# One core, a decoder layer in split fp32: the order of the first transfers, more work on two chunks behind the norms, and a second SwiGLU whose combinations read x from DRAM

## The chip, the cores and the metric

The kernel runs on one core of a Trainium2 chip. The time is device microseconds of one execution; below it is the median of three runs. The core has a matrix engine (PE, with its weight loads shown as PEld), a vector engine (DVE), a scalar engine (ACT), a third general engine (POOL), and an engine that mostly issues DMAs (SP). ACT and POOL issue DMAs too. Each engine takes its own instructions strictly in order and waits for the others by semaphores.

## The reference, cut to what matters

One step of a one-layer hybrid decoder for a prompt of 1024 tokens and 8 single-token samples that share the weights:

```python
def swiglu(x, w1, w3, w2):
    return (jax.nn.silu(x @ w1) * (x @ w3)) @ w2

def decoder_layer(x, ...):
    x = layer_norm(ALPHA * x + 0.5 * swiglu(x, ffn1_w1, ffn1_w3, ffn1_w2), ln1_g, ln1_b)
    m, st = hybrid_mixer(x, ...)      # x @ w_in -> RG-LRU and gated DeltaNet -> @ w_o
    x = layer_norm(ALPHA * x + m, ln2_g, ln2_b)
    x = layer_norm(ALPHA * x + 0.5 * swiglu(x, ffn2_w1, ffn2_w3, ffn2_w2), ln3_g, ln3_b)
    return x, st
```

x is 1032 x 1024, the hidden width of a SwiGLU is 2816, all in float32. The mixer's projection w_in gives, among others, K, Q and V of eight heads of 128, each followed by a causal convolution over time and a SiLU, and two gates per head.

## The kernel before, in words

**Number format and tiles.** Features lie on the 128 partitions, tokens along the free axis. The 1032 tokens are three chunks of 344 (`NT`, `TC`); the 1024 features are eight k-tiles (`KD`). A float32 operand is split into a rounded half and the rest (`split`: ACT writes the first, DVE or POOL subtracts): x into `XH`, `XL`, weights into `wh`, `wl`. Each product takes three matmuls per k-tile (`mm3`), so one output tile of 128 x 344 is a group of 24 matmuls.

**A SwiGLU** (`ffn`, run with n = 1 and n = 2) has 22 f-tiles of 128 hidden features. The first two (`FIRST`) are *plain*: w1 and w3, three chunks, 6 groups, 144 matmuls. Tiles 2 to 20 use *Strassen*: 7 products instead of 8 on blocks of 128 x 258, 168 matmuls. These need four linear combinations of quarters of x, split again into `CH` and `CL` (`combos`, four rounds k = 0 to 3). A round makes four tiles of x (`G`, or `u` and `si`) as XH + XL, one addition of 128 x 516 each on POOL, combines them on DVE, and splits the results (ACT, then DVE). `CL` lies in the memory of `ACC`. The tiles of a f-tile's result go to DRAM (`gs`, from POOL's queue) and are read back for w2. Tile 21 is plain, in the second half.

**The start.** `x_load(t)` loads the eight k-tiles of one chunk of x into `ACC` and splits them; chunk 0 from ACT's queue, chunks 1 and 2 from SP's, where the weights are loaded as well (`wload`, raw tiles of 128 x 512, three buffers).

**A norm** (class `LN`) runs per chunk in three steps: sums by matmuls with ones (`ps_sq`) give the mean and then the variance, and the last step scales and shifts and writes XH and XL. Four of the eight k-tiles (`ON_POOL`) are subtracted on POOL. The last chunk of a norm meets the stage that follows: `fin` is stepped from inside the mixer's first projections (`kqv_first`) and from the first plain tile of the second SwiGLU.

**The mixer** begins with K and Q of head 0 on chunks 0 and 1, then the gates' projections (`ab`), then chunk 2; then `gates()`, and V's three chunks behind it. Then come eight heads (`gdn`), with the projections of the next head as filler between them (`stream`). In head 0 the part that inverts a triangular matrix (line 848) is the next place with long dependencies. The order on each engine comes from the order in which the code is written, with a scheduler that moves instructions of one engine past one another unless they are pinned (`keep_in_program_order`).

**Beside the second SwiGLU** run sixteen jobs on the samples' states (`states`): two loads from POOL's queue each, four scalings on ACT and four on DVE.

## Time and profile before

| what | value |
|---|---|
| median of 3 runs | 2636.21 us (2635.96 to 2637.09) |
| the profiled execution | 2637.03 us, span of its instructions 2635.1 us |
| PE busy | 2535.4 us, 96% of the span |
| DVE, ACT, POOL busy | 1784.2, 1133.9, 493.8 us |
| chain that ended last | PE 80%, DVE 9%, ACT 7% of the span |
| granted TensorE clock, mean | 0.984 |

The span is the time from the first to the last instruction; the profiled execution's own time is 1.9 us longer. "Busy" of PE says that matmuls were in flight, also when the granted clock was low, so it is an upper bound of useful work. The page's forty slices are 65.9 us each.

### The profile page before, as it was taken

How to read it: one execution, taken by the hardware profiler on the slowest of the kernel's cores; microseconds unless marked ns; L12 is line 12 of the kernel's file. 1: busy time of each engine (PE TensorE's matmuls, PEld its weight loads, DVE VectorE, ACT ScalarE, POOL GpSimd, SP SyncE). 2: the span in 40 equal slices, each digit the busy share in tenths (PEclk: the TensorE clock that was granted, in tenths of full speed). 3: DMA queues.
4: the chain of work that ended last, by engine and by line, in shares of the span. 5: the costliest groups of instructions: out<-in, count | busy, mean ns of one | idle time of the engine just before them, and what ended most of it. 6: DMA issues, size and time to landing. Idle time of an engine off the chain costs nothing.

```text
span 2635.1 us, 47251 instructions
## 1 busy us (share of the span) xinstructions
PE 2535.4 (96%) x18398; PEld 2486.9 (94%) x18398; DVE 1784.2 (68%) x3657; ACT 1133.9 (43%) x2419; POOL 493.8 (19%) x612
## 2 busy tenths in 40 slices
PE   7999999999989999999999999999699999999996
PEld 7999999999979999999999999989699999999996
DVE  7766665645589676777767686767786666666446
ACT  4433333312363737465564637634533333332125
POOL 5000000300332021111112021144521111021013
PEclk8999999999989999999999999999899999999998
DMA  4222222423101121111211121123314444333221
GB/s 140 78 77 82 80 76 70 125 79 113 41 26 51 34 56 43 39 48 34 57 37 53 34 56 36 52 87 117 83 66 112 118 123 119 93 112 110 81 69 65
DMA packets 146816, 195.98 MB, mean 74 GB/s; under 512 B 34720, under 2 KB 75680, under 8 KB 146592
## 3 DMA queue, kind: packets, MB, share of 16 engines
q1 hardware_dynamic: 125024, 154.13, 19.3%
q0 software_dynamic: 10160, 32.06, 4.7%
q10 hardware_dynamic: 11408, 6.77, 0.9%
q8 instruction: 145, 2.38, 0.4%
q14 instruction: 79, 0.65, 0.1%
HBM read 156.15 MB, written 36.76 MB: 73 GB/s over the span
## 4 chain that ended last, share of the span: by engine, by line
PE 80%; DVE 9%; ACT 7%; issue 2%; POOL 1%; DMA 1%; ACTq 0%; SPq 0%; POOLq 0%; DVEq 0%
PE ps_mm L130 32%; PE ps_g L130 11%; PE ps_g L287 10%; PE ps_mm L287 10%; PE ps_sq L287 8%; ACT L88 2%; DVE ACC L94 2%; PE ps_g L848 2%; PE ps_sq L734 2%; DVE ACC L91 1%; ACT lnq L88 1%; DVE wl L91 1%; PE ps_g L734 1%; PE ps_g L740 1%; DMA ACC<-x 1%
## 5 line engine op out<-in xcount | busy, mean ns | idle before, releaser
L130 PE MATMUL ps_mm<-XH,wh 128*128 128x344 f32 x1680 | 568.9, 339 | 11.0 <-ACT XH L88 7.0
L130 PE MATMUL ps_mm<-XL,wh 128*128 128x344 f32 x1680 | 542.2, 323 | 6.2 <-POOL XL L91 6.1
L130 PE MATMUL ps_mm<-XH,wl 128*128 128x344 f32 x1680 | 542.7, 323 | 4.6 <-DVE wl L91 4.6
L88 ACT ACTIVATE wh<-wraw 128x512 fp32r<-128x512 f32 (+2 forms) x366 | 217.8, 599 | 423.2 <-PE ps_mm L130 155.4
L130 PEld LDWEIGHTS ps_mm<-XH,wh 128*128 128x128 f32 x1680 | 320.6, 191 | 15.3 <-ACT XH L88 7.6
L130 PEld LDWEIGHTS ps_mm<-XL,wh 128*128 128x128 f32 x1680 | 320.7, 191 | 8.9 <-POOL XL L91 6.9
L130 PEld LDWEIGHTS ps_mm<-XH,wl 128*128 128x128 f32 x1680 | 320.0, 190 | 5.7 <-DVE wl L91 5.6
L91 DVE TENSOR_TENSOR wl<-wraw,wh 128x512 fp32r<-128x512 f32 (+3 forms) x345 | 246.4, 718 | 52.5 <-ACT wh L88 47.4
L287 PE MATMUL ps_g<-CH,wh 128*128 128x258 f32 x760 | 214.7, 283 | 0.0
L287 PE MATMUL ps_g<-CH,wl 128*128 128x258 f32 x760 | 214.6, 282 | 0.0
L287 PE MATMUL ps_g<-CL,wh 128*128 128x258 f32 x760 | 214.3, 282 | 0.0
L88 ACT ACTIVATE wh<-S 128x512 fp32r<-128x512 f32 x152 | 95.8, 631 | 201.0 <-PE ps_sq L287 129.3
L287 PE MATMUL ps_mm<-XH,wl 128*128 128x258 f32 x608 | 171.5, 282 | 0.7 <-DVE wl L91 0.7
L287 PE MATMUL ps_mm<-XH,wh 128*128 128x258 f32 x608 | 171.8, 282 | 0.5 <-ACT wh L88 0.5
L287 PE MATMUL ps_mm<-XL,wh 128*128 128x258 f32 x608 | 171.3, 282 | 0.0
L342 POOL DMA_DIRECT2D gs<-G x76 | 41.5, 546 | 666.1 <-DVE G L91 618.9
L91 DVE TENSOR_TENSOR wl<-S,wh 128x512 fp32r<-128x512 f32 x152 | 105.0, 691 | 69.4 <-ACT wh L88 69.0
L287 PEld LDWEIGHTS ps_g<-CL,wh 128*128 128x128 f32 x760 | 143.5, 189 | 0.0
L287 PEld LDWEIGHTS ps_g<-CH,wh 128*128 128x128 f32 x760 | 143.2, 188 | 0.0
L287 PEld LDWEIGHTS ps_g<-CH,wl 128*128 128x128 f32 x760 | 143.1, 188 | 0.0
L88 ACT ACT_TABLE_LOAD x109 | 139.8, 1283 | 6.1 <-issue 3.3
L130 PE MATMUL ps_g<-gl,wh 128*128 128x344 f32 x444 | 142.1, 320 | 0.0
(503 smaller groups left out, 6872.5 us busy)
## 6 DMA issues: line engine op xcount, KB each, us to landing
wraw<-w SPq DMA_DIRECT2D x164, 256.0 KB, 2.8
wraw<-w_in SPq DMA_DIRECT2D x128, 256.0 KB, 2.6
gr<-gs SPq DMA_DIRECT2D x84, 258.0 KB, 2.8
gs<-G POOLq DMA_DIRECT2D x76, 258.0 KB, 2.6
wr<-w SPq DMA_DIRECT2D x76, 256.0 KB, 2.6
wraw<-w_o SPq DMA_DIRECT2D x40, 256.0 KB, 2.7
y<-ACC SPq DMA_DIRECT2D x32, 129.0 KB, 1.9
d<-lt SPq DMA_DIRECT2D x8, 512.0 KB, 3.3
```

The costliest lines, as they stand in the source:

```text
L88: return S.activation(out, in_, f, **kw)
L91: return (eng or V).tensor_tensor(out, a, b, op=op)
L94: return V.scalar_tensor_tensor(out, a, s, b, op0=op0, op1=op1)
L130: PE.matmul(p, a, b, start=(n == 0), stop=(n == 3 * nk - 1))
L287: PE.matmul(ps_[c], a[:, k, :], b, start=(start and n == 0), stop=(n == 11), skip_group_check=not start)
L342: G.dma_start(gs[f][:, s], x)
L734: x = PE.matmul(ck(p, i), a, b, start=True, stop=True)
L740: x = PE.transpose(ck(p, i), a, IDT)
L848: pin(PE.matmul(o[r, c, :], a(c), b(c), start=True, stop=True))
```

## The change

Three places are edited.

*Start of the first SwiGLU.* Chunk 0 of x is issued alternately from ACT's and POOL's queue; w1 and w3 of tile 0 are issued on SP ahead of chunks 1 and 2, pinned; w3's raw tiles come from the buffers `wr`, which the Strassen tiles use later; the splits of x are separated from its loads. The rounds of `combos` no longer add XH and XL: they load x from DRAM, rounds 0 and 1 from SP, rounds 2 and 3 from POOL's queue.

*Start of the mixer.* V of head 0 joins K and Q: its weights wait in the tiles `hM`, `hP`, `hLT`, `hP2`, and its convolution's input lies in the tile `lt`.

*Second norm and second SwiGLU.* The last step of the second norm writes y = the full x on ACT for all eight k-tiles, splits it, and stores it to DRAM (`X2`) from POOL's queue. `FIRST` becomes 3 for n = 2, so tile 2 is plain. Tiles 0 and 1 run on chunks 0 and 1 first, then both on chunk 2; tile 1's weights wait in the tiles of `S`, `wr`, `s0` and `rb`. The rounds of `combos` load x from `X2` on POOL's queue. What is left of the samples' jobs after the last Strassen tile is run there.

```diff
--- before.py
+++ after.py
@@ -25,7 +25,7 @@
 LN_EPS = 1e-5
 RMS_EPS = 1e-6
 NF = 22
-FIRST, LASTF = 2, 21
+FIRST, LASTF = {1: 2, 2: 3}, 21
 GROUPS = [[21, 0, 1], [2, 3, 4], [5, 6, 7, 8], [9, 10, 11, 12], [13, 14, 15, 16], [17, 18, 19, 20]]
 TH_ = T // 2
 TQ = T // 4
@@ -105,18 +105,20 @@
 
     LNB = {"s1": 3, "mu": 1, "s2": 2, "lnq": 3}
 
-    def wload(src, nk, m=128, eng=None, hold=None):
+    def wload(src, nk, m=128, eng=None, hold=None, raws=None, pin=False):
         hl = []
         for k0 in range(0, nk, 4):
             n = min(4, nk - k0)
             pad = [128, 512 // m, m]
-            raw = wp.tile([128, n, m], F32, name="wraw", tag="wraw", bufs=3, padded_shape=pad)
+            raw = raws() if raws else wp.tile([128, n, m], F32, name="wraw", tag="wraw", bufs=3, padded_shape=pad)
             if hold:
                 h, l = hold(n)
             else:
                 h = wp.tile([128, n, m], F32R, name="wh", tag="wh", bufs=4, padded_shape=pad)
                 l = wp.tile([128, n, m], F32R, name="wl", tag="wl", bufs=4, padded_shape=pad)
-            nc.sync.dma_start(raw, src[:, k0:k0 + n])
+            x = nc.sync.dma_start(raw, src[:, k0:k0 + n])
+            if pin:
+                tc.keep_in_program_order(x)
             split(h, l, raw, eng)
             hl += [(h[:, k, :], l[:, k, :]) for k in range(n)]
         return hl
@@ -140,10 +142,15 @@
 
     def x_load(t):
         for k in range(KD):
-            (nc.sync if t else nc.scalar).dma_start(ACC[:, k, ts(t)], A["x"][:, k, ts(t)])
+            q = nc.sync if t else (nc.scalar, G)[k % 2]
+            tc.keep_in_program_order(q.dma_start(ACC[:, k, ts(t)], A["x"][:, k, ts(t)]))
+
+    def x_split(t):
+        for k in range(KD):
             split(XH[:, k, ts(t)], XL[:, k, ts(t)], ACC[:, k, ts(t)])
 
     exps = []
+    X2 = dr.tile([128, KD, T], F32, name="x2")
 
     class LN:
         def __init__(self, gi, s, out=None, tail=False):
@@ -218,9 +225,11 @@
                     nc.sync.dma_start(self.out[:, k, self.s], y)
                     continue
                 h, l = XH[:, k, self.s], XL[:, k, self.s]
-                if i in ON_POOL:
+                if i in ON_POOL or self.gi == 2:
                     act(y, y, AF.Identity, bias=b_)
-                    split(h, l, y, G)
+                    split(h, l, y, G if i in ON_POOL else V)
+                    if self.gi == 2:
+                        G.dma_start(X2[:, k, self.s], y)
                     continue
                 act(h, y, AF.Identity, bias=b_)
                 stt(l, y, b_, h.bitcast(F32), OP.add, OP.subtract)
@@ -232,7 +241,7 @@
         split(h, l, raw)
         return h, l
 
-    def combos(up):
+    def combos(up, x_src, early):
         CH_ = up.tile([128, 4, 4, TH_], F32R, name="CH")
         CL = big.tile([128, 4, 4, TH_], F32R, name="CL", tag="A")
         yield CH_, CL
@@ -244,7 +253,9 @@
             x1a, x1b, x2a, x2b = b
             for x, r, h in ((x2b, k + 4, 1), (x1b, k, 1), (x1a, k, 0), (x2a, k + 4, 0)):
                 c = slice(h * TH_, (h + 1) * TH_)
-                tt(x, XH[:, r, c].bitcast(F32), XL[:, r, c].bitcast(F32), OP.add, G)
+                d = (nc.sync if k < early else G).dma_start(x, x_src[:, r, c])
+                if k < early:
+                    tc.keep_in_program_order(d)
             tt(x2b, x2b, x1b, OP.subtract)
             tt(x1b, x1a, x1b, OP.subtract)
             stt(x1a, x2b, -1.0, x1a, OP.mult, OP.subtract)
@@ -341,15 +352,22 @@
         def store(f, s, x):
             G.dma_start(gs[f][:, s], x)
 
-        def plain(f, put, after=None):
-            a1 = wload(w1[f], KD)
-            if n == 1 and f == 0:
+        def weights(f, hold=None, raws=None):
+            first = n == 1 and f == 0
+            if first:
                 x_load(0)
-            a3 = wload(w3[f], KD)
-            for t in range(NT):
+            a1 = wload(w1[f], KD, hold=hold, pin=first)
+            if first:
+                x_split(0)
+            return a1, wload(w3[f], KD, hold=hold, raws=raws if first else None, pin=first)
+
+        def plain(f, put, after=None, w=None, chunks=range(NT), raws=None):
+            a1, a3 = w or weights(f, raws=raws)
+            for t in chunks:
                 s = ts(t)
                 if n == 1 and f == 0 and t:
                     x_load(t)
+                    x_split(t)
                 p1 = psum("mm")
                 mm3(p1[:, :TC], a1, xsl(t), KD)
                 if fin and f == 0 and t < 2:
@@ -365,10 +383,14 @@
 
         with pool("ffna%d" % n) as up:
             extra = side(up)
-            make = combos(up)
+            make = combos(up, *((A["x"], 2) if n == 1 else (X2, 0)))
+            spare = ["S"] * 3 + ["wr"] * 3 + ["s0", "rb"]
+
+            def held(n):
+                return [up.tile([128, n, 128], F32R, name="w1" + x, tag=x, bufs=3 if x in ("S", "wr") else 2) for x in (spare.pop(), spare.pop())]
             for f in range(LASTF):
-                if f < FIRST:
-                    def put(s, p1, p3):
+                if f < FIRST[n]:
+                    def put(s, p1, p3, f=f):
                         si = third()
                         act(si, p1, AF.Silu)
                         stt(si, si, -1.0, p3, OP.mult, OP.mult)
@@ -381,11 +403,27 @@
                         if f or t == NT - 1:
                             next(make, None)
                     cx = None if f == 0 else cx
-                    plain(f, put, after)
+                    ahead = None if n == 1 or f < 2 else ahead
+                    if n == 1 or f > 1:
+                        plain(f, put, after, ahead, raws=lambda: up.tile([128, 4, 128], F32, name="wr", tag="wr", bufs=3))
+                    elif f == 0:
+                        first = (weights(0), put)
+                        plain(0, put, None, first[0], range(2))
+                    else:
+                        w = weights(1, hold=held)
+                        plain(1, put, None, w, range(2))
+                        plain(0, first[1], None, first[0], range(2, NT))
+                        ahead = weights(2)
+                        cx = next(make)
+                        next(make)
+                        plain(1, put, None, w, range(2, NT))
+                        next(make)
                 else:
                     strassen(f, w1, w3, up, cx, store)
                     for _ in range(NT):
                         next(extra, None)
+            for _ in extra:
+                pass
 
         with pool("ffnb%d" % n) as up:
             ACC = big.tile([128, KD, T], F32, name="ACC", tag="A")
@@ -567,7 +605,7 @@
             B4 = [128, 4, 128]
 
             def full(tag, n=T):
-                return mp.tile([128, n], F32, name=tag, tag=tag, padded_shape=[128, T])
+                return mp.tile([128, n], F32, name=tag, tag=tag, padded_shape=[128, 3 + T if tag == "lt" else T])
 
             def eight(tag):
                 return full(tag, TP).rearrange("p (c j) -> p c j", j=128)
@@ -587,8 +625,8 @@
             def ck(x, c):
                 return x[:, c * 128:(c + 1) * 128]
 
-            def pre_tile():
-                pre = mp.tile([128, 3 + T], F32, name="pre", tag="pre", bufs=2)
+            def pre_tile(tag="pre"):
+                pre = mp.tile([128, 3 + T], F32, name="pre", tag=tag, bufs=2 if tag == "pre" else 1)
                 G.memset(pre[:, :3], 0.0)
                 return pre
 
@@ -646,13 +684,18 @@
 
             def kqv_first():
                 dst = kqv_dst(0)
+                spare = ["hM", "hP", "hLT", "hP2"]
+
+                def hold(n):
+                    return [mp.tile([128, n, 128], F32R, name="wv", tag=spare.pop()) for _ in range(2)]
                 wk, wq = (wload(A["w_in"][b0], KD) for b0 in (KC, QC))
-                evs = [silu_evac(d, pre_tile(), b0) for d, b0 in zip(dst, (KC, QC))]
+                wv = wload(A["w_in"][VC], KD, hold=hold)
+                evs = [silu_evac(d, pre_tile(x), b0) for d, b0, x in zip(dst, (KC, QC, VC), ("pre", "pre", "lt"))]
                 ab = gates_proj()
 
                 def kq(t, i):
                     p = psum("mm")
-                    mm3(p[:, :TC], (wk, wq)[i], xsl(t), KD)
+                    mm3(p[:, :TC], (wk, wq, wv)[i], xsl(t), KD)
                     evs[i][1](t, p[:, :TC])
 
                 kq(0, 0)
@@ -662,17 +705,18 @@
                 next(fin)
                 next(fin)
                 kq(1, 1)
+                kq(0, 2)
+                kq(1, 2)
                 ab(0)
                 ab(1)
                 ab(2)
                 kq(2, 0)
                 kq(2, 1)
+                kq(2, 2)
                 gates()
                 for t in range(NT):
                     for e in evs:
                         e[2](t)
-                for _ in proj(VC, silu_evac(dst[2], pre_tile(), VC)[0]):
-                    pass
                 KQV[0] = dst
 
             GG = mp.tile([128, 9, H], F32, name="GG")
@@ -1065,7 +1109,7 @@
                         for tag in tags:
                             n = 1 if tag[0] in "hr" else 3
                             x = mp.tile([128, n * TC], F32R, name="m_" + tag, tag=tag, bufs=2 if tag == "pre" else 1,
-                                        padded_shape=[128, 512] if tag[0] == "h" else [128, TC] if n == 1 else [128, 3 + T] if tag == "pre" else [128, T])
+                                        padded_shape=[128, 512] if tag[0] == "h" else [128, TC] if n == 1 else [128, 3 + T] if tag in ("pre", "lt") else [128, T])
                             ap += [x[:, i * TC:(i + 1) * TC] for i in range(n)]
                         yield ap
 
```

The new order on SP at the program's start. Before (`wraw` are weight tiles, `ACC<-x` the transfers of x for chunks 1 and 2, `wr` weights of the first Strassen tile):

```order
L119 DMA wraw<-w_1 128x512 x3
L143 DMA ACC<-x 128x344 x6
L119 DMA wraw<-w_1 128x512
L143 DMA ACC<-x 128x344 x10
L119 DMA wraw<-w_1 128x512 x3
L261 DMA wr<-w_1 128x512 x3
```

and now (`G`, `si`, `u` are the tiles of x for `combos`):

```order
L119 DMA wraw<-w_1 128x512 x2
L119 DMA wr<-w_1 128x512 x2
L146 DMA ACC<-x 128x344 x16
L256 DMA G<-x 128x516 x4
L119 DMA wraw<-w_1 128x512 x3
L272 DMA wr<-w_1 128x512 x3
```

All four weight tiles of f-tile 0 now precede x of chunks 1 and 2, and the first loads for `combos` stand between x and the weights of f-tile 1.

POOL in the last chunk of the second norm and behind it. Before (`s` are the norm's sums, `gs` results to DRAM):

```order
L91 TENSOR_TENSOR s_20870<-s_20870,lnq 128x344 x3
L342 DMA gs<-lnq 128x344
L91 TENSOR_TENSOR u_21168<-XH,XL 128x516
L91 TENSOR_TENSOR u_21167<-XH,XL 128x516
L91 TENSOR_TENSOR XL<-ACC,XH 128x344 x2
L91 TENSOR_TENSOR G<-XH,XL 128x516 x2
L91 TENSOR_TENSOR XL<-ACC,XH 128x344
```

and now (`x_77` is `X2`):

```order
L353 DMA gs<-lnq 128x344
L232 DMA x_77<-ACC 128x344 x2
L91 TENSOR_TENSOR XL<-ACC,XH 128x344
L232 DMA x_77<-ACC 128x344 x2
L256 DMA u_21337<-x_77 128x516
L91 TENSOR_TENSOR XL<-ACC,XH 128x344
L232 DMA x_77<-ACC 128x344 x2
L91 TENSOR_TENSOR XL<-ACC,XH 128x344
L232 DMA x_77<-ACC 128x344 x2
```

The additions are gone; in their place stand the stores of x, two ahead of each subtraction that writes XL, and a load that reads x back, on the same queue.

On PE, 105 matmuls stood between the sum of the first norm's last variance and the gates' transposes; now 171 do (3 of Q, 48 of V, 48 of the gates, 48 of K and Q, 24 of V). From the transposes to the first matmul of line 848 there were 347, now there are 300.

DVE at the first round of `combos` in the second SwiGLU, now (`wl<-wraw,wh` are the splits of f-tile 2's weights):

```order
L94 SCALAR_TENSOR_TENSOR lnq<-lnq,ps_g 128x344
L91 TENSOR_TENSOR G<-G 128x516
L91 TENSOR_TENSOR CL<-G,CH 128x516
L91 TENSOR_TENSOR G<-G 128x516
L94 SCALAR_TENSOR_TENSOR G<-G 128x516
L91 TENSOR_TENSOR si<-si,u_21337 128x516
L94 SCALAR_TENSOR_TENSOR G<-G 128x516
L91 TENSOR_TENSOR CL<-G,CH 128x516
L94 SCALAR_TENSOR_TENSOR lnq<-lnq,ps_g 128x344
L91 TENSOR_TENSOR CL<-G,CH 128x516 x2
L91 TENSOR_TENSOR u_21337<-u_21336,u_21337 128x516
L91 TENSOR_TENSOR wl<-wraw,wh 128x512
```

The splits of f-tile 2's weights come behind the instructions of the first two rounds that take the loaded x, on an engine that keeps this order.

## The prediction

> **What bounds the kernel now.** I read the page's busy shares, its 40 slices and the chain first, then the stretches in which the tenths of PE fall, with the waits and the chain of each.
>
> ```profile
> PE 2535.4 (96%) x18398; PEld 2486.9 (94%) x18398; DVE 1784.2 (68%) x3657; ACT 1133.9 (43%) x2419; POOL 493.8 (19%) x612
> PE   7999999999989999999999999999699999999996
> PEclk8999999999989999999999999999899999999998
> 0.00:74.00 74.00, 56.26 (x293) 53.42 (x294) 55.94 (x78) 33.93 (x67) 36.44 (x36) 0.88 0.40 127
> 756.00:776.00 20.00, 14.03 (x66) 9.34 (x64) 17.90 (x32) 14.93 (x27) 6.19 (x6) 0.81 0.00 1
> 776.00:782.00 6.00, 5.96 (x21) 5.26 (x22) 1.99 (x4) 1.50 (x3) 0.00 (x0) 0.50 0.00 0
> 788.00:848.00 60.00, 60.00 (x409) 59.06 (x407) 56.08 (x151) 24.86 (x77) 17.62 (x23) 1.00 0.21 55
> 1870.00:1945.00 75.00, 56.69 (x295) 53.79 (x295) 64.68 (x81) 35.31 (x62) 38.47 (x34) 0.86 0.24 65
> ```
>
> The page's row of engines comes first. PE is busy for 2535.4 of 2635.1 us, so only its holes can be won. Three tenths are low: the start, the place around 760, and around 1870 to 1945. The last five rows are time windows: busy us of PE, weight loads, DVE, ACT and POOL, granted clock, DMA share, GB/s. The change touches just these holes. A hole costs twice: PE idles, and after it the granted clock is 0.50 (776 to 782), so that a "busy" PE does half the work. I therefore count matmuls, not busy time, and price them at full clock:
>
> ```profile
> 27.45 3.77 PE ps_g L130 x24
> 73.60 2.89 PE ps_mm L287 x22
> 1944.56 2.88 PE ps_mm L287 x24
> 1964.77 2.87 PE ps_mm L287 x24
> ```
>
> These are pieces of the chain (start, length, what). L130 is a plain matmul, L287 one of Strassen's. Twenty-four matmuls of a plain group take 3.77 us, 0.157 each. A Strassen f-tile takes 1964.77 - 1944.56 = 20.2 us, a plain one 6 x 3.77 = 22.6.
>
> **Part 1, the start.** The two plain f-tiles ahead of the first Strassen tile are 288 matmuls, 45.2 us, yet Strassen starts at 73.60: 28.4 us are lost. Where?
>
> ```profile
> 0.73 3.87 DMA ACC<-x
> 11.34 5.08 DMA ACC<-x
> 33.64 8.41 DVE wl L91
> 43.38 0.69 DVE wl L91
> 15.00:21.00 6.00, 5.40 (x18) 4.81 (x18) 4.55 (x9) 4.36 (x10) 0.00 (x0) 0.52 0.99 335
> PE ps_mm L130 <- ACT XH L88: 7.0, 2, 6.5
> L91 POOL TENSOR_TENSOR G<-XH,XL 128x516 f32<-128x516 f32 x8 | 11.4, 1446 | 4.5 <-DVE CL L91 4.5
> 32.74 5.06 POOL L91 TENSOR_TENSOR G<-XH,XL 128x516 f32<-128x516 f32 x4
> ```
>
> The last transfer of x for chunk 0 lands at 16.4, and PE's longest wait (6.5) is for its XH; from 15 to 21 the DMA share is 0.99 and the clock 0.52. Chunk 0's two groups were done by 23.7 (the group at 27.45 follows one of 3.77), where 48 matmuls are worth 7.5: 16 of the 28 us. The other 12 go later: one weight split on DVE took 8.41 us instead of 0.69 while POOL ran its XH + XL additions (32.74 to 41.5), and the combinations trail on DVE to 72.9.
>
> The change has x(0) issued from two queues at once, w1 and w3 ahead of everything on SP, and x(1), x(2) behind them. Chunk 0 of x is 1.4 MB, w1 and w3 1.05 MB each: 3.5 MB, of which w1 and x(0) (2.4) let PE begin. At the 335 GB/s of the row above 2.4 MB take 7.3 us, w3 3 more; a first transfer took 3.87 us to land, so the first group starts at 10 to 12 and both end by 16 to 18 (partly at half clock). The other 240 matmuls add 37.7: Strassen at 54 to 57, if nothing else waits. The 16 POOL additions disappear (8 of G at 1446 ns and 8 alike), and with them what stood beside the 8.41 us split; in their place come 16 loads of 258 KB. By Strassen's start x (4.2 MB), three f-tiles of weights (2.1 each) and these loads (4.1) make 14.6 MB, 44 us at 335 GB/s: inside the 54, narrowly. I take **17.5 us** gained; bounds 10 (transfers late) and 20.
>
> **Part 2, the mixer's first projections.** The hole of 756 to 776:
>
> ```profile
> 760.70 0.85 PE ps_sq L169 x2
> 787.53 0.61 PE ps_g L707 x8
> PE ps_sq L169 <- DVE s L91: 5.5, 3, 2.6
> PE ps_mm L699 <- DVE XL L94: 2.9, 2, 2.2
> 776.04 0.49 PE ps_mm L699
> 843.41 0.64 PE L848 MATMUL ps_g<-IC,hLT 128*64 128x16 f32 x8
> ```
>
> From the norm's second sum (760.70) to the gates' transposes (787.53) PE issues 105 matmuls (counted in the order of instructions), some 16.5 us, in 26.8: 10 lost. The change puts 72 V matmuls there. Of these 48 stand ahead of the third chunk's gates (DVE wl, then XL at about 776 to 777), worth 7.5 us; the hole fills, the clock stays up, and the gates come at about 788 as before, but with V's 72 matmuls (11.3 us) behind them instead of ahead. The splits of wv add two DVE instructions of 0.69 us to the norm's way.
>
> Does it carry on? Behind the gates DVE is 56.08 of 60 us busy until head 0's inverse begins (843.41). In the new order 300 matmuls (47 us) lie between those two points instead of 347, so PE would be there at 835; DVE is spared only the convolutions of V's first two chunks (5 instructions of 0.4 to 0.6 us each, 5 us in all), so it arrives near 840 to 843, and PE stalls again. What is left at that point is the gain at 843.41 (1 to 4 us) and 25 matmuls done in advance (3.9 us), which may be missed as filler in the inverse. I take **5 us**; bounds 0 and 8.5.
>
> **Part 3, the second norm and the second SwiGLU.** The first tile starts near 1870.5, Strassen at 1944.56: 74 us for 288 matmuls (45.2), 29 lost.
>
> ```profile
> PE ps_sq L169 <- DVE s L91: 6.7, 1, 6.7
> PE ps_mm L130 <- POOL XL L91: 6.1, 3, 3.2
> PE ps_mm L130 <- ACT wh L88: 4.0, 1, 4.0
> PE ps_g L130 <- DVE wl L91: 3.8, 1, 3.8
> 1873.48 7.75 DMA s<-S
> 1902.66 3.10 POOL G L91 x2
> 1908.80 5.28 DVE G L91
> L91 POOL TENSOR_TENSOR G<-XH,XL 128x516 f32<-128x516 f32 x8 | 12.6, 1588 | 2.9 <-DVE G L94 1.9 <-DVE XL L94 0.9
> gs<-lnq POOLq DMA_DIRECT2D x6, 172.0 KB, 2.2
> s<-S POOLq DMA_DIRECT2D x2, 256.0 KB, 5.9
> rb<-rtd POOLq DMA_DIRECT2D x2, 256.0 KB, 8.1
> L342 POOL DMA_DIRECT2D gs<-lnq x5 | 2.8, 564 | 10.1 <-DVE lnq L94 10.1
> 1908.85 0.92 POOL L91 TENSOR_TENSOR XL<-ACC,XH 128x344 fp32r<-128x344 f32 x1
> ```
>
> Four waits of 1864 to 1945 make 20.6 us; the rest is mostly clock (0.86 on average). The norm of chunk 2 is late (its mean waits on ACT behind work on the sample state, whose load took 7.75), its last XL is written from 1908.85 to 1909.8, and POOL's additions hold the splits up again (5.28 us for a subtraction).
>
> *Order of work.* f-tiles 0 and 1 now run on chunks 0 and 1 first: 192 matmuls, 30.1 us, that need nothing of chunk 2, against 96 before. With a stall of about 3.5 us for the variance instead of 6.7, they end at 1870.5 + 30.1 + 3.5 + 2 to 3 of low clock, 1906 to 1908. Chunk 2 was complete at 1909.8 with POOL's additions in the way; without them and with the mean some 4 us earlier I expect 1902 to 1904. So no wait. Chunk 2 of both (96, 15.1 us) ends at about 1923.
>
> *Price.* f-tile 2 becomes plain: 22.6 - 20.2 = 2.4 us, certain. Its 144 matmuls are the cover for the combinations, so Strassen starts at about 1945.5 with three tiles done, where before it had done two and would be through the third at 1964.77: **19 us**, the 2.4 paid.
>
> *What the change adds.* On POOL 24 stores of 172 KB, 564 ns to issue (13.5 us over three norms), and 16 loads. ACT gets 4 more instructions of about 0.5 us per chunk. The second sample-state job is no longer loaded ahead (its tiles hold weights), two issues less on POOL. The trace does not show a store of x read back. From below: issue 0.56 plus 2.2 to land, twice, 5.6 us; from above 8.1 us, as the bunched transfers took, twice: 16. In order on DVE, f-tile 2's weight splits stand behind the first combination rounds. With the last store issued at 1902 to 1904, loads land at 1906 to 1908 by the lower price; a round is 8 instructions of 0.69, 5.5 us; the splits are ready from 1913 to 1920, needed from 1923. The slack is 4 to 6 us; by the upper price Strassen comes some 5 us later, and if the norm is slow too, 13. I take the lower (same queue, same size: 2.2 us) and knock 0.5 off: **18.5 us**, bounds 5 and 22.
>
> *Against it.* POOL's transfers landed in 2.2 us here while DVE was busy 64.68 of 75 us. The Trainium skill, "SBUF — State Buffer", section "SBUF: two separate sides", warns (the 'DVE blocks DMA' trap) that GpSimd itself writes the descriptors of a transfer on its queue and is locked out while DVE runs in a two-port mode, so that the transfer seems to wait for DVE. By that rule the sum would be that of rival 4; the trace so far does not bear it out, since 2.2 us leaves little room for it.
>
> **The sum.** The profiled execution took 2637.03 us (span 2635.1), 0.8 above the median of the runs, 2636.21. 2637.03 - 17.5 - 5 - 18.5 = **2596**.
>
> **The rivals.**
>
> 1. *The round trip through DRAM eats part 3.* Stores and loads share POOL's queue with the norm's XL; bunched transfers took 8.1. For it: CL's first write waits for all stores. Against: 2.2 us. Part 3 falls to about 5: 2609.5.
> 2. *The start is bound by transfers.* 14.6 MB ahead of Strassen are 44 us, so every gap in the queues pushes it back. For it: a share of 0.99 at 15 to 21. Against: the second f-tile's weights and x(1), x(2) make 9.5 MB with all that comes before them, 28 us, and are wanted at 33. Part 1 falls to 10: 2603.5.
> 3. *V only moves the stall.* DVE at 56.08 of 60; part 2 gives 0: 2601.
> 4. *POOL's descriptors wait for DVE.* The last 16 transfers each held for one DVE instruction (0.69): 11 us, of which 4 to 6 is slack; +6: 2602. Against: the same 2.2 us.
> 5. *Slower.* DVE runs in order, so the first combination instruction that waits for a load of x holds all weight splits behind it, in each of four rounds. To lose the 41 us gained and 5 more, each round would have to wait 46 / 4 = 11.5 us beyond its slack of about 4, so loads of over 15 us against 2.2, or 8.1 at worst: over 2642.
>
> **How the numbers follow.** Forecast 0.62, rival 1 0.14, rival 2 0.11, rival 3 0.07, rival 4 0.03, rival 5 0.03. The forecast's own range is 2586 (all three terms at their best ends, 2.5 + 3.5 + 3.5 us) to 2604 (one term short by 8). Rivals 2 to 4 lie inside it or at its edge, rival 1 just beyond, so 2584 to 2611, with 2 us to spare below, leaves out rival 5 and two rivals together: under 2 in 10. What a measurement can tell from no change is 0.2%, 5.3 us: faster is below 2631. All but rival 5 and some mishap of two rivals together are there: faster 0.94, same 0.03, slower 0.03.
>
> **What the changed profile would show.** Part 1: the first matmul before 12, no DVE split over 2 us before 60, Strassen's first group at 54 to 58; a first matmul at 15 or waits on wraw tell of rival 2. Part 2: no clock of 0.50 at 758 to 764 (776 to 782 less part 1's gain); PE waiting for DVE by 4 to 8 us ahead of the inverse (L848, now L892); if by 11, rival 3. Part 3: no wait of the plain groups on XL, no POOL addition of XH and XL, Strassen at f = 3 about 74 to 77 us behind the first tile; DVE waiting for G or u loads over 6 us, and PE for wl behind it, mean rival 1. A POOL store at 2 to 3 us in the stretch denies rival 4. The forecast is wrong if the three starts of Strassen and of the inverse come at these times and the end does not.

## The result and the profile after

The changed kernel takes 2613.16 us (median of five runs, 2610.70 to 2623.99) against 2637.09 us for the kernel before on the same chip (2635.96 to 2639.72): a ratio of 0.9918, 95% interval 0.9896 to 0.9940. That is 24 us where 41 were forecast, and outside the range of 2584 to 2611. The profiled execution took 2612.26 us, span 2610.5. The runs below were made on four chips, on which the kernel before took 2636.2 to 2638.3 us; each ratio is against the kernel before on the same chip.

The page after (busy shares, tenths of PE and clock), and windows at the places that the prediction quoted (the columns are as there):

```profile
PE 2532.2 (97%) x18374; PEld 2485.7 (95%) x18374; DVE 1742.9 (67%) x3641; ACT 1134.0 (43%) x2426; POOL 467.4 (18%) x633
PE   9999999999999999999999999998799999999996
PEclk9999999999998999999999999999899999999998
...
0.00:55.00 55.00, 48.80 (x292) 47.15 (x293) 42.34 (x82) 34.63 (x68) 15.37 (x32) 1.00 0.77 254
756.00:776.00 20.00, 20.00 (x133) 18.17 (x132) 17.69 (x40) 8.70 (x21) 1.88 (x6) 1.00 0.17 53
776.00:836.00 60.00, 55.55 (x362) 53.25 (x361) 48.85 (x135) 21.59 (x67) 14.83 (x21) 0.94 0.16 44
1861.00:1941.00 80.00, 72.22 (x438) 70.98 (x437) 51.98 (x90) 40.78 (x76) 31.02 (x44) 0.94 0.54 158
```

Two of the three holes are gone: the start does its 288 matmuls in 55 us, and PE is busy for all of 756 to 776. But the stretch of head 0, which had 60.00 of 60 before, now has 55.55, and the last row holds 442 matmuls by the order of instructions, worth 69 us at 0.157 each, in 80. To see what each place gave, I read the start of the same PE instruction in both traces:

| place, first matmul of | before | after | ahead of before by |
|---|---|---|---|
| the first Strassen tile | 72.36 | 54.54 | 17.8 |
| the first norm's first sum | 702.69 | 684.04 | 18.7 |
| the first norm's last variance | 760.70 | 743.34 | 17.4 |
| the gates' transposes | 787.46 | 772.52 | 14.9 |
| head 0's inverse (L848, now L892) | 843.41 | 828.31 | 15.1 |
| the RG-LRU's gates behind it ("rX") | 866.10 | 852.01 | 14.1 |
| the last head's sum of squares ("kt") | 1814.58 | 1800.27 | 14.3 |
| the second SwiGLU | 1867.69 | 1861.04 | 6.7 |
| Strassen at f = 3 | 1964.61 | 1941.14 | 23.5 |

(The prediction's 1964.77 is the same place as the chain counts it.) So part 1 gave 18.7 us (forecast 17.5), part 2 took 4.5 away in this profile (forecast +5), and part 3 gave 23.5 - 14.3 = 9.2 (forecast 18.5). About 1 us more comes behind. All later runs are read by two measures from this table: **head 0**, how far "rX" lies ahead of 866.10, and **norm 2**, the time from "kt" to Strassen at f = 3, 150.0 before and 140.9 after.

Head 0 has to be read with care. Seven kernels share the mixer of the change (the change, e2, e3, e5, e6, e7 and e13), and in their profiles "rX" lies 13.5 to 19.5 us ahead. The change's 14.1 is near the worst of them. Most of that scatter arises between the inverse and "rX", as the last section tells; at the inverse itself the seven lie 15.1 to 17.6 us ahead.

**The start** is now one row of groups behind the first transfers. From the chain after (start, length, what):

```profile
2.15 8.72 DMA ACC<-x
...
11.99 1.06 PE ps_mm L132 x5
13.05 3.79 PE ps_g L132 x24
...
50.94 3.77 PE ps_g L132 x24
54.70 2.87 PE ps_mm L298 x24
```

The chain holds only the end of the first group. The first matmul of all is this row of PE's timeline:

```profile
5.81 0.66 PE L132 MATMUL ps_mm<-XH,wh 128*128 128x344 f32 x1 [5.81 <-ACT wh L88]
```

**Head 0.** The waits of PE from 740 to 860 (sum, times, longest), then pieces of the chain there, and two windows, from the gates to the inverse before and after:

```profile
PE ps_sq L176 <- DVE s L91: 2.5, 1, 2.5
PE ps_g L778 <- DVE kt L91: 1.9, 1, 1.9
PE ps_g L892 <- DMA IC<-d: 1.4, 1, 1.4
PE ps_g L812 <- POOL gu L91: 1.1, 3, 0.5
```

```profile
784.62 2.61 POOL gu L91 x2
...
795.06 1.89 POOL nh L91
...
799.56 3.77 DMA d<-lt
803.74 4.08 DMA BL<-d
...
823.40 2.16 DMA d<-X
825.62 2.56 DMA IC<-d
828.31 1.20 PE ps_g L892 x16
```

```profile
787.50:843.40 55.90, 55.90 (x376) 55.20 (x375) 51.61 (x144) 24.27 (x74) 16.48 (x22) 1.00 0.21 56
772.50:828.30 55.80, 51.36 (x329) 49.47 (x329) 46.16 (x136) 22.00 (x69) 12.71 (x21) 0.97 0.17 47
```

From the gates to the inverse 828.31 - 772.52 = 55.8 us pass; before it was 843.41 - 787.46 = 55.95, with 47 matmuls (7.4 us) more between them. Before, PE was busy for all of it, so its own matmuls already filled the distance. After, PE idles for 4.4 us and at the end waits for a transfer, so PE's work no longer sets it. DVE is busy for only 46.16 of the 55.8 us. What is left is a row of steps that each wait for the one before, many of them short ones on DVE, with four transfers to and from DRAM in it (12.6 us). Its length hardly depends on PE's work: from the gates to the issue of the first transfer of `IC` it is 52.8 us before and 53.1 after, and 51.9 to 53.2 in the other eight kernels that project K and Q of chunk 2 ahead of the gates.

**The second norm.** The waits of PE from 1800 to 1945, rows of PE's timeline (the wait ahead of an instruction stands in brackets), and ACT's timeline around chunk 2's mean:

```profile
PE ps_sq L176 <- DVE s L91: 10.9, 3, 7.6
PE ps_g L132 <- DVE wl L91: 4.4, 2, 4.1
```

```profile
1828.30 0.84 PE L176 MATMUL ps_sq<-s,ONES 128*128 128x344 f32 x2 [3.14 <-DVE s L91]
1830.74 0.66 PE L132 MATMUL ps_mm<-m_pre,wl 128*128 128x344 f32 x1 [1.59 <-POOL wl L91]
...
1850.71 0.66 PE L132 MATMUL ps_g<-m_pre,wl 128*128 128x344 f32 x1 [4.08 <-DVE wl L91]
...
1881.13 1.51 PE L176 MATMUL ps_sq<-s,ONES 128*128 128x344 f32 x2 [7.59 <-DVE s L91]
```

```profile
1865.18 0.61 ACT L88 ACTIVATE w1wr<-wraw 128x512 fp32r<-128x512 f32 x1
1871.38 0.63 ACT L88 ACTIVATE w1wr<-wraw 128x512 fp32r<-128x512 f32 x1 [5.58 <-DMA wraw<-w]
1871.91 0.44 ACT L88 ACTIVATE mu<-ps_sq 128x344 f32<-128x344 f32 x1
```

Behind the last variance nothing stops PE: some 360 matmuls follow one another from 1881 to 1941, with no wait for a load of x, none for POOL. The waits all lie ahead of it. The sums for chunk 2's mean start at 1865.16, but ACT, in order, stands at a split of f-tile 1's weights (`w1wr`) until their transfer lands; the mean (`mu`) is copied at 1871.91, and PE waits 7.59 us for the variance. The chain and the DMA issues of that place say why the weights are late:

```profile
1864.09 7.27 DMA wraw<-w
```

```profile
wraw<-w SPq DMA_DIRECT2D x11, 256.0 KB, 3.0
x<-ACC POOLq DMA_DIRECT2D x7, 172.0 KB, 2.2
rb<-rtd POOLq DMA_DIRECT2D x1, 256.0 KB, 7.4
s<-S POOLq DMA_DIRECT2D x1, 256.0 KB, 8.1
```

The median weight load takes 3.0 us; this one took 7.27, while the two loads of the first sample-state job were under way. That they share something is the suspicion that the runs below test.

### The profile page after: what moved, and what is told of

It is laid out like the page before. It is cut to its first block, busy times and chain, and to the rows that moved or that the text cites. A ratio compares the mean times of both kernels' runs of the same rounds, so it can differ in the third digit from the quotient of the medians.

```text
span 2610.5 us, 47260 instructions
## 1 busy us (share of the span) xinstructions
PE 2532.2 (97%) x18374; PEld 2485.7 (95%) x18374; DVE 1742.9 (67%) x3641; ACT 1134.0 (43%) x2426; POOL 467.4 (18%) x633
## 4 chain that ended last, share of the span: by engine, by line
PE 83%; ACT 6%; DVE 6%; DMA 1%; issue 1%; POOL 1%; ACTq 0%; SPq 0%; DVEq 0%; POOLq 0%
PE ps_mm L132 34%; PE ps_g L132 13%; PE ps_g L298 10%; PE ps_mm L298 10%; PE ps_sq L298 8%; PE ps_g L892 2%; ACT L88 2%; DVE ACC L94 2%; PE ps_sq L778 2%; ACT lnq L88 1%; PE ps_g L778 1%; PE ps_g L784 1%; DVE ACC L91 1%; POOL s L91 1%; DVE wl L91 1%
## 5 line engine op out<-in xcount | busy, mean ns | idle before, releaser
L132 PE MATMUL ps_mm<-XH,wh 128*128 128x344 f32 x1656 | 558.3, 337 | 6.1 <-ACT wh L88 5.8
L132 PE MATMUL ps_mm<-XH,wl 128*128 128x344 f32 x1656 | 532.9, 322 | 0.0
L132 PE MATMUL ps_mm<-XL,wh 128*128 128x344 f32 x1656 | 532.6, 322 | 0.1
L88 ACT ACTIVATE wh<-wraw 128x512 fp32r<-128x512 f32 (+2 forms) x360 | 213.9, 598 | 408.8 <-PE ps_mm L132 140.9
L132 PEld LDWEIGHTS ps_mm<-XH,wh 128*128 128x128 f32 x1656 | 314.4, 190 | 9.6 <-ACT wh L88 5.8
L132 PEld LDWEIGHTS ps_mm<-XL,wh 128*128 128x128 f32 x1656 | 314.4, 190 | 1.8 <-DVE XL L91 0.6
L132 PEld LDWEIGHTS ps_mm<-XH,wl 128*128 128x128 f32 x1656 | 313.8, 190 | 0.4 <-DVE wl L91 0.2
L91 DVE TENSOR_TENSOR wl<-wraw,wh 128x512 fp32r<-128x512 f32 (+3 forms) x339 | 232.3, 688 | 42.5 <-ACT wh L88 38.4
L132 PE MATMUL ps_mm<-gl,wh 128*128 128x344 f32 x444 | 142.0, 320 | 0.0
L132 PE MATMUL ps_g<-gh,wh 128*128 128x344 f32 x444 | 142.0, 320 | 0.0
L132 PE MATMUL ps_mm<-gh,wh 128*128 128x344 f32 x444 | 142.0, 320 | 0.0
```

The lines of the kernel that those rows point to most:

```text
L88: return S.activation(out, in_, f, **kw)
L91: return (eng or V).tensor_tensor(out, a, b, op=op)
L132: PE.matmul(p, a, b, start=(n == 0), stop=(n == 3 * nk - 1))
```

## The experiments

### Which part gave what

**e1** is the change without the edit of the mixer (its main lines; `...` marks what is left out):

```diff
-                wv = wload(A["w_in"][VC], KD, hold=hold)
...
-                kq(0, 2)
-                kq(1, 2)
...
-                kq(2, 2)
...
+                for _ in proj(VC, silu_evac(dst[2], pre_tile(), VC)[0]):
+                    pass
```

**e8** is the kernel before with part 1 alone. Against e1 it has the old order of the second SwiGLU, no stores of x, and POOL's additions there (`x_src` is None for n = 2):

```diff
-FIRST, LASTF = {1: 2, 2: 3}, 21
+FIRST, LASTF = {1: 2, 2: 2}, 21
...
-                    if i in ON_POOL or self.gi == 2:
+                    if i in ON_POOL:
...
-                        G.dma_start(X2[:, k, self.s], y)
...
+                if x_src is None:
+                    tt(x, XH[:, r, c].bitcast(F32), XL[:, r, c].bitcast(F32), OP.add, G)
+                    continue
...
-                    if n == 1 or f > 1:
+                    if n == 1 or f < 9:
```

> The kernel before with the first edit alone (order of the first transfers, x loaded for the first combinations). Strassen's first group at 54 to 55 instead of 73 in both chains: 18 to 19 us won, and 2617 to 2619 if nothing later gives any of it back.

> The changed kernel with its mixer edit undone (V of head 0 behind the gates again). The forecast's own term says 5 us are lost: 2618. Chain theory (the gates start a chain of fixed length, 55.9 us in both kernels, to head 0's inverse; V's 72 matmuls push the gates 3.5 us back and are missing as cover afterwards): 4 to 5 us are won, 2608 to 2609. If head 0 has nothing to do with the loss, 2613.

e8: 2617.48 us, ratio 0.9925 (0.9910 to 0.9939), 20 us by the medians; head 0 is 20.0 ahead. e1: 2610.67 us (2609.99 to 2612.22), 0.9902 (0.9887 to 0.9917); head 0 19.9 ahead, norm 2 143.7. So part 1 is worth 18 to 20 us and carries through the mixer undiminished if V is left where it was. Part 3 is worth 6 to 7 us (e1 against e8: 6.8 by the medians, 6.1 by norm 2). The edit of the mixer costs something: the medians of e1 and the change differ by 2.5, less than the change's own scatter, and head 0 stands 5.8 us better without it. Against all seven kernels with this edit that is 0.4 to 6.4 us at "rX" and 2.6 to 5.1 at the inverse, so a loss is clear only at the inverse.

### Why V in advance lost: the place of the gates

If the distance from the gates to the inverse is a chain of steps, the fault of the edit is that 24 matmuls of V, and K and Q of chunk 2 as before, stand ahead of the gates. **e4** is the change with the gates called as soon as their projections are done. **e12** makes the same edit in e1, so without V in advance.

```diff
                 ab(2)
+                gates()
                 kq(2, 0)
                 kq(2, 1)
                 kq(2, 2)
-                gates()
```

> The changed kernel with the gates' transposes and their vector work moved ahead of chunk 2 of K, Q and V. Chain theory: the gates come some 11 us earlier, the inverse follows at the same 56 us, PE has 72 matmuls of cover behind the gates: 8 to 12 us won, 2601 to 2605. DVE theory (DVE's throughput, 56 of 60 us busy, sets the inverse): the same DVE instructions, no gain, 2611 to 2614.

> The change without its edit of the mixer, and the gates ahead of K and Q of chunk 2. It tells whether V in advance is worth anything once the gates are first. Theory of the chain (only the place of the gates counts, V is filler either way): the end of the inverse's stretch 22 to 24.5 us earlier than before (24.1 with V in advance), time 2605 to 2608. Forecast's view (V fills 7.5 us of a hole in the first norm that nothing else fills): the stretch ends 17 to 19 us earlier, time 2610 to 2612.

e4: 2605.61 us, ratio 0.9884 (0.9869 to 0.9899). The gates come at 759.73 instead of 772.52, the inverse at 818.80, and head 0 is 24.1 ahead. DVE has the same work, so its work in all does not fix when the inverse can begin. e12: 2616.61 us, 0.9916 (0.9901 to 0.9931), head 0 only 15.5 ahead: here the theory of the chain missed by 6.5 us and more, and the forecast's view of the hole (17 to 19) was nearer, though it missed too.

| head 0 ahead of before by | gates behind K, Q (V) of chunk 2 | gates first |
|---|---|---|
| V behind the gates | 19.9 (e1), 20.0 (e8) | 15.5 (e12) |
| V in advance | 14.1 (the change), 13.5 to 19.5 in seven kernels | 24.1 (e4), 18.9 to 24.1 in seven kernels (e4, e9 to e11, e14 to e16) |

At the inverse, ahead of most of the scatter, the four cells do not overlap except the two poor ones: 20.1 and 20.2 us ahead (e8, e1), 16.0 (e12), 15.1 to 17.6, and 21.1 to 25.1. So the two edits need each other. Without V in advance, PE has nothing to do while the norm finishes chunk 2, in e1 (4.0 us) as in e12. The waits of PE in e12 and in e4 in this stretch:

```profile
PE ps_mm L737 <- DVE XL L94: 3.9, 3, 2.4
```

```profile
PE ps_sq L176 <- DVE s L91: 0.9, 1, 0.9
```

V fills that hole, as forecast, and costs nothing as long as the gates do not stand behind it. The way from the gates to the inverse is 69 us in e12 and 59 in e4 instead of 56, so the gates are not always where the chain starts: with the gates first, K and Q of chunk 2 stand behind them. DVE's last instruction on them, in e1 and in e12:

```profile
774.21 0.49 DVE L94 SCALAR_TENSOR_TENSOR kq<-lnq,kq 128x336 f32<-128x336 f32 x1
```

```profile
778.24 1.37 DVE L94 SCALAR_TENSOR_TENSOR kq<-lnq,kq 128x336 f32<-128x336 f32 x1
```

It starts 4.0 us later in e12, and the inverse comes 4.2 us later. From it to the issue of `IC` it is 45.9 us before, 46.2 in e1 and 46.6 in e12. So without V in advance the time seems to count from K and Q, and these are not ready sooner for having the gates first. In e12 they are even later, with a granted clock of 0.50 from 758 to 766 where e1 has 0.63 and 1.00; why in e12 is open.

### The second norm: four edits that moved a wait

The mean of chunk 2 is late, and the scheduler put chunk 1's variance 41 matmuls behind its mean instead of 97, where PE waits 3.14 us for it. **e2** pins the variances where they are written, **e5** puts the mean and the squares ahead of f-tile 1's splits on ACT. **e6** issues the stores of x from ACT, **e7** has no stores and adds XH and XL on POOL as e8 does, **e3** has no stores and loads the input x instead. The edits of e2 (`pin` is set for the variances of the second norm), of e5 (the squares, and the splits of f-tile 1's weights, are pinned in the same way), of e6, and of e3:

```diff
             for i, x in enumerate(xs):
-                PE.matmul(p, ONES, x, start=(i == 0), stop=(i == len(xs) - 1))
+                y = PE.matmul(p, ONES, x, start=(i == 0), stop=(i == len(xs) - 1))
+                if pin:
+                    tc.keep_in_program_order(y)
```

```diff
-            act(mu, pm, AF.Copy, scale=1.0 / D)
+            z = act(mu, pm, AF.Copy, scale=1.0 / D)
+            if self.gi == 2:
+                tc.keep_in_program_order(z)
```

```diff
-                        G.dma_start(X2[:, k, self.s], y)
+                        nc.scalar.dma_start(X2[:, k, self.s], y)
```

```diff
-                        G.dma_start(X2[:, k, self.s], y)
...
-            make = combos(up, *((A["x"], 2) if n == 1 else (X2, 0)))
+            make = combos(up, A["x"], 2 if n == 1 else 0)
```

> The changed kernel with the variance matmul of the second norm pinned to its written place, 97 matmuls behind the mean instead of 41. Order theory (the variance of chunk 1 moved ahead, PE waits 3.1 us for it and its last step then holds the splits of w_o on DVE, 4.1 us): the first group of the second SwiGLU comes 5 to 7 us earlier, 2606 to 2608. Store theory (the stores of x on POOL's queue slow DVE and POOL there): no change, 2612 to 2614.

> The changed kernel with one order on ACT changed: in the second norm's last chunk the mean and the squares are pinned ahead of the splits of f-tile 1's weights (now the mean stands behind a split that waits 5.6 us for its weights). ACT theory (that in-order wait makes the norm late): 4 to 6 us won, 2607 to 2609, the variance 5 us earlier. If the norm is held by DVE, POOL or the stores: 2612 to 2614.

> The changed kernel without the 24 stores of x; the second SwiGLU's combinations load the kernel's input x in their place (same size, wrong data), so nothing waits for a store. Store theory: 5 to 7 us are won ahead of the second SwiGLU, 2606 to 2608. Order theory: at most 1 to 2 us, 2611 to 2613. Rival 1 of the forecast (the round trip through memory delays the combinations): the last groups ahead of Strassen have no wait to lose, so also 2611 to 2613.

> The changed kernel with the 24 stores of x issued from ACT's queue instead of POOL's. Leaving the stores out won about 4 us. If it was POOL's time for the issues (0.56 us each): about the same here, 2609 to 2611. If it was the traffic or the waits for landing: no gain, 2612 to 2614. If ACT pays for 24 issues of 0.45 us on the norm's way: 2615 to 2618.

> The changed kernel with the new order of the second SwiGLU, but x for its combinations again made by 16 additions on POOL, and the norm's last step as before (no stores, no loads). The forecast's part 3: the additions hold up splits on DVE (5.3 us for one) and run into the cover of f-tile 2: 2616 to 2622. If the order alone brings the gain and the stores cost what the additions cost: 2610 to 2614.

| | us, median (range) | ratio (95%) | norm 2 | chunk 2's variance behind "kt" |
|---|---|---|---|---|
| the change | 2613.16 (2610.70 to 2623.99) | 0.9918 (0.9896 to 0.9940) | 140.9 | 80.9 |
| e2 | 2612.26 (2611.16 to 2613.70) | 0.9909 (0.9893 to 0.9926) | 141.1 | 81.2 |
| e5 | 2611.51 (2608.32 to 2619.47) | 0.9906 (0.9888 to 0.9924) | 142.8 | 74.9 |
| e3 | 2609.20 (2604.99 to 2613.18) | 0.9896 (0.9879 to 0.9912) | 136.6 | 77.6 |
| e6 | 2615.92 (2605.96 to 2620.39) | 0.9912 (0.9886 to 0.9938) | 142.1 | 83.0 |
| e7 | 2610.11 (2606.46 to 2616.59) | 0.9899 (0.9883 to 0.9915) | 143.7 | 76.8 |

None is told from the change by its interval. e2 starts the second SwiGLU 5 us earlier from "kt", but only two of its matmuls. They stand ahead of the last ten of the output projection, and behind them PE waits for a split of that projection's weights:

```profile
1856.42 0.66 PE L132 MATMUL ps_mm<-m_rX,wl 128*128 128x344 f32 x1 [4.74 <-POOL wl L91]
```

The projection's last matmul starts 63.5 us behind "kt" in e2 and 60.6 in the change, so the pin wins nothing. e5 has the variance 6 us earlier, and then this row of PE:

```profile
1887.33 0.66 PE L134 MATMUL ps_g<-XH,w1S 128*128 128x344 f32 x1 [7.65 <-DVE w1S L91]
```

The last of f-tile 1's weights are split only at 1885.25, behind a scaling of the sample state that waited 2.95 us for its load, and the norm's last step behind that. Both edits treat an order; neither touches what is late. e6's runs spread over 14 us and tell nothing.

e7 is no faster or slower by its interval, but its profile shows an exchange. The output projection's last matmul starts 51.6 us behind "kt" where the change has 60.6 (and e3, without the stores alone, 56.6). Chunk 2's variance comes 4.1 us earlier. But from this variance to Strassen at f = 3 it needs 66.9 us where the change needs 60.0. There PE waits, as the forecast's part 3 said of the additions, for the splits of f-tile 2's weights:

```profile
PE ps_mm L132 <- DVE wl L91: 2.7, 1, 2.7
PE ps_mm L132 <- ACT wh L88: 2.1, 1, 2.1
```

So the additions have a price here, and it is hidden in the sum by what the norm's old last step wins ahead of the first tile.

### The first state loads

Two theories were left: W, that ACT takes weights and norm in the wrong order, and D, that the weights' transfers are slowed by the state loads. **e9** is e4 with the mean first and the weights' splits in an order written out; **e10** is e4 with the state loads held back until chunk 2 is normalized; **e11** is both; **e13** is the change itself with the state loads held back. The edit of e9 against e4, beside e5's lines:

```diff
-                        plain(0, put, None, first[0], range(2))
+                        plain(0, put, None, first[0], range(1))
+                        w = weights(1, hold=held)
+                        plain(0, put, None, first[0], range(1, 2))
                     else:
-                        w = weights(1, hold=held)
                         plain(1, put, None, w, range(2))
```

And of e10 against e4, the same for e11 against e9 and for e13 against the change: a dummy takes the tiles of the first state job, and POOL frees them by a sum with XH of chunk 2.

```diff
+            def occupy():
+                d = [up.tile([128, 4, 128], F32, name="d" + x, tag=x, bufs=2) for x in ("s0", "rb")]
+                for x in d:
+                    G.memset(x[:, 0, :4], 0.0)
+                return d
+
+            def release(d):
+                for x in d:
+                    tt(x[:, 0, :4], x[:, 0, :4], XH[:, KD - 1, T - 4:].bitcast(F32), OP.add, G)
...
                         w = weights(1, hold=held)
+                        hel = occupy()
                         plain(1, put, None, w, range(2))
                         plain(0, first[1], None, first[0], range(2, NT))
+                        release(hel)
                         ahead = weights(2)
```

> The version with the gates first (2605.6 us), and in the second norm the mean and the squares stand ahead of the splits of f-tile 1's weights on ScalarE, these splits in the order written, called between chunk 0 and chunk 1 of f-tile 0, so ahead of the scalings of the sample state. Theory W (what part 3 lacks is lost because f-tile 1's weights and chunk 2's norm take turns in the wrong order on ScalarE): from kt (L1277) to Strassen at f = 3 136 to 139 us instead of 143.6, time 2599 to 2602. Theory D (the weights are late because their transfers share the queues with the first state loads): nothing moves by more than 1.5 us, 2604 to 2607, and PE waits for ACT or DVE splits whose own wait is for wraw.

> The version with the gates first, and the two loads of the first state job held back behind chunk 2 of the norm (their tiles are first taken by a dummy that POOL frees by a sum with XH of chunk 2). Theory D: the load of f-tile 1's weights takes 4 to 5 us instead of 7.3, the mean of chunk 2 comes 3 us or more earlier, kt to Strassen at f = 3 138 to 140, time 2600 to 2602. Theory W: the order on ScalarE is the same, so at most 1.5 us are gained: 2604 to 2606.

> Both of these edits together. If both causes are real the gains add: kt to Strassen at f = 3 132 to 136, time 2595 to 2599. If one of them alone is the cause, this run is within 1.5 us of the run with that one.

> The change with nothing but the first state loads held back behind chunk 2 of the second norm. If the state loads are the cause, kt (L1277) to Strassen at f = 3 goes from 140.9 to 134 to 137, time 2606 to 2610. If the 7 us of the earlier run came with the gates' place, 139.5 to 142 and 2611 to 2615.

| | us, median (range) | ratio (95%) | norm 2 |
|---|---|---|---|
| e4 | 2605.61 (2604.84 to 2608.20) | 0.9884 (0.9869 to 0.9899) | 143.6 |
| e9 | 2603.22 (2602.86 to 2603.91) | 0.9868 (0.9853 to 0.9883) | 133.0 |
| e10 | 2599.42 (2598.62 to 2601.58) | 0.9856 (0.9839 to 0.9872) | 136.8 |
| e11 | 2599.14 (2596.36 to 2601.50) | 0.9852 (0.9837 to 0.9866) | 132.9 |
| e13 | 2605.97 (2601.21 to 2609.40) | 0.9882 (0.9868 to 0.9897) | 136.6 |

ACT's timeline, the same split in e4 and in e10:

```profile
1863.78 0.63 ACT L88 ACTIVATE w1wr<-wraw 128x512 fp32r<-128x512 f32 x1 [5.56 <-DMA wraw<-w]
```

```profile
1859.19 0.63 ACT L88 ACTIVATE w1wr<-wraw 128x512 fp32r<-128x512 f32 x1 [0.43 <-DMA wraw<-w]
```

The order on ACT is the same in both, and the wait falls from 5.56 to 0.43 us with the two loads moved away, while the longest load of these weights falls from 7.8 to 4.3 us: D is shown for this wait. (The same edit moves the first job's scalings on ACT and DVE out of the norm's way, so the 6.8 us in norm 2 need not be the transfers' alone.) The Trainium skill, "DMA: Bandwidth & Descriptors", section "Issuing engines are not separate DMA queues", says that transfers begun by the scalar, sync or GpSimd engine all run on the same 16 DMA engines and interleave; the 7.27 us of a weight load on SP's queue beside two loads from POOL's, against 3.0, agrees. e13 shows the same step on the change itself: norm 2 falls by 4.3 us. The medians fall by 7.2, of which a part may be head 0, 19.5 us ahead in e13 and 14.1 in the change.

W is not shown by e9, though norm 2 falls there by 10.6 us, because e9's edit moves the loads too. POOL issues the first of them here, in e4 and in e9:

```profile
1855.28 0.79 POOL L1309 DMA_DIRECT2D rb<-rtd  x1
```

```profile
1868.89 0.79 POOL L1316 DMA_DIRECT2D rb<-rtd  x1
```

That is 65.3 and 75.1 us behind "kt", and three of f-tile 1's four weight tiles are loaded in e9 by then. This fits with gains that do not add: e11 holds the loads back further and stands at 132.9, no better than e9. What tells of W alone is e11 against e10, with the loads away in both: 3.9 us in norm 2, and nothing in the medians. Nor does e9 keep its 10.6. Some 3.9 us were lost ahead of "kt", where its edit changes nothing, and from Strassen's start to the last matmul of the program e9 needs 662.4 us against 657.9 in e4. PE's waits from 1930 in e9:

```profile
PE ps_mm L304 <- DVE wl L91: 3.3, 1, 3.3
```

The first Strassen tile now begins before its own weights are split. e9, e10 and e11 beat both kernels by a clear interval; which of e10 and e11 is better can't be told.

### What is left

**e14** is e10 with e3's edit, **e15** is e10 with e2's pinned variances, **e16** is e11 with them. First the line that e14 drops, then the edit of e15 and e16:

```diff
-                        G.dma_start(X2[:, k, self.s], y)
```

```diff
-            self.total(pv, parts)
+            self.total(pv, parts, self.gi == 2)
```

> Gates first, state loads held back (2599.4 us, kt to Strassen 136.8), and no stores of X2: the combinations load the input x, so the second SwiGLU works on wrong data from there. If the 4 us that the stores cost came from sharing the DMA queues with state loads and weights at the same time, 135.3 to 137.5 and 2598 to 2600. If the stores cost by themselves (POOL's issue, the round trip), 132 to 133.5 and 2594.5 to 2596.

> Gates first, state loads held back, and the sums of the second norm's variances pinned where they are written. Before, with the state loads in the way, the first tile came 5 us earlier and the variance of chunk 2 took it back. If that was due to the state loads, kt to Strassen is 131 to 133.5 and the time 2594 to 2597; if chunk 2's chain takes it back in any case (the same latency from its sums), 136 to 138 and 2599 to 2601.

> All edits together: gates first, state loads held back, variances pinned, f-tile 1's weights in the order written with the mean and the squares ahead of them. If all act, kt to Strassen is 127 to 131; if the weights of the first Strassen tile then come too late (3.3 us with the order on ScalarE alone), the gain stops there: 131 to 134 and 2596 to 2599.

e14: 2602.21 us, ratio 0.9869 (0.9854 to 0.9883), norm 2 139.1: not better than e10, so the 4 us that e3 seemed to show were no price of the stores that reaches Strassen. e15: 2603.45 us, 0.9877 (0.9861 to 0.9894), norm 2 138.5; e16: 2601.80 us, 0.9868 (0.9853 to 0.9883), norm 2 137.2. Pinning made nothing better. PE's waits in e15 from 1785 to 2010 have at the top one for splits of the output projection's weights on POOL, which e2 shows too (5.6 and 4.7 us):

```profile
PE ps_mm L132 <- POOL wl L91: 9.8, 2, 5.1
```

That leaves the 7.7 us lost ahead of the first tile (265 matmuls from "kt" in both traces, 53.1 us before, 60.8 after). The place of chunk 1's variance is not what costs them, though e15 and e16 were built on that: pinned, the output projection's last matmul comes later, 66.2 us behind "kt" in e15 against 61.4 in e10. With the norm's last step as before and no stores it comes at 51.6 (e7), in the kernel before at 48.8. So the time goes to the new last step and its stores. Which of their instructions hold up the projection's splits was not tested.

## Why the prediction was wrong, step by step

**Part 1 was right, its first step by luck.** The first group did not start at "10 to 12" but at 5.81, and its 24 matmuls took until 12.9; "the first matmul before 12" was no sign at all, since the kernel before started at 6.54. Both groups of chunk 0 ended at 16.8 (forecast 16 to 18), Strassen came at 54.5 (54 to 57), 18.7 us instead of 17.5. No single split takes DVE over 2 us, and by 56 us 14.1 MB had moved, close to the 14.6 of the estimate. Rival 2 would have shown waits on raw weights; there are none behind the first.

**Part 2 had the wrong sign.** The hole was filled as said: PE is busy for 20.00 of 20 us at a clock of 1.00. The failing step is "Behind the gates DVE is 56.08 of 60 us busy until head 0's inverse begins". I took a busy share of 93% for a bound of throughput, and did not ask what V ahead of the gates costs. In the runs it is a chain of steps that counts from the gates where K and Q of chunk 2 are projected ahead of them: 52.8 us to the issue of `IC` before, 53.1 after. So two things count, where the gates stand and whether enough filler is left behind them. The gates came at 772.5, where "about 788 as before" less the 17.5 of part 1 says 770.5, and where e1, without V, has them at 767.2. The first matmul of the inverse came at 828.3 where 822.5 to 825.5 was forecast. The "25 matmuls done in advance" were worth 2 us at best: from the inverse to "rX" 22.7 us before, 20.6 to 20.7 in e2, e3 and e13, but 23.7 in the change at a clock of 0.71. "PE waiting for DVE by 4 to 8 us ahead of the inverse" came in size only, 4.4 us between the gates and the inverse; at the inverse it is 1.4, for a transfer. Over the seven kernels with this mixer the term lies between 5 us lost and 1 won, never at the 5 won of the forecast. The question I left out was what the moved work is put ahead of; e4 is the answer, 9.5 us better at the inverse.

**Part 3 had the right mechanism and half the size.** As forecast there is no wait on XL, none for the combinations, and no addition on POOL. The loads of x took 4.0 us in the median where 2.2 was taken, and DVE waited up to 3.5 us for a loaded G (the mark for rival 1 was 6), hidden in front of PE:

```profile
DVE CL L91 <- ACT CH L88: 5.3, 2, 4.5
DVE G L91 <- DMA G<-x: 3.8, 2, 3.5
```

From the first tile to Strassen at f = 3 the change needs 80.1 us, where "74 to 77" was said (from 1870.5, which is 2.8 us behind the first matmul) and the kernel before needed 96.9: 16.8 gained in that stretch. The term was mis-sized by two steps. The first: "with the mean some 4 us earlier". I had seen that the mean waits on ACT behind work on the sample state, with a load of 7.75 us in the quoted row, and gave no reason for an earlier mean but that the second state job is no longer loaded ahead. The first one still is, now beside f-tile 1's weights, whose splits the change moved ahead of the mean on the same engine; the variance came 5.3 us later from "kt" than before (80.9 against 75.6) instead of earlier. The edits that free it win 4.3 (e13) to 10.7 us (e11 against e4). The other is that the forecast took the way to the first tile as unchanged, and 7.7 us went there. It had listed what the norm's new last step adds (stores, and more instructions on ACT), but charged it to the combinations alone; e7, without it, ends the output projection 9 us earlier. At chunk 2's variance the two weigh about the same: 3.1 us earlier in e13, 4.1 in e7.

**The rivals.** Rival 1 had part 3 at about 5, and 9.2 was measured, but its reason was not there: e14, without the stores, is no better than e10, and PE waited for no load of x. Rival 3 (part 2 gives 0) was nearest in kind, too mild for the change's profile and about right for e2, e3, e5 and e13. Rival 4 is denied by the sign set for it: all 24 stores landed in a median of 2.2 us with DVE busy for 51.98 of 80 us; the trap that the Trainium skill describes on "SBUF — State Buffer", section "SBUF: two separate sides", did not show here; whether DVE was in a two-port mode no run shows. Rival 5 was far off.

## What to carry to other kernels

Before work is moved into a hole, name what it is put ahead of: if a long chain of steps starts behind it, the chain's first instruction goes in front and the moved work becomes its cover; a busy share, even 93%, does not tell a chain from a bound. And when a transfer is put on the path, list every other transfer issued in the same few microseconds, on any queue, and every instruction behind its consumer on an in-order engine: two loads for work that could wait cost 4 to 7 us through one split of weights.
